# Two blocks in one kernel: layer-norm sums on ScalarE, lower parts and routing in another order, four experts combined on the chip

## The chip, the cores and the metric

The kernel runs on one core of a Trainium2 chip, in one launch. The metric is device microseconds of one execution; shown is the median of three runs. The engines are TensorE (PE in the rows, its weight loads PEld), VectorE (DVE), ScalarE (ACT), GpSimd (POOL) and SyncE (SP, which issues most of the DMAs). Arrays are 128 partitions by columns.

## The reference

512 tokens of 1024 numbers pass through two transformer blocks. Block 1 ends with two layer norms and a mixture of 16 experts between them; block 2 is an attention block with RMS norms and ends with 32 experts.

```python
# block 1, from its attention on
x = layer_norm(ALPHA * x + mixed, ln1_g[l], ln1_b[l])
ffn = hier_moe(x, ...)                       # 16 experts, 2 for a token
x = layer_norm(ALPHA * x + ffn, ln2_g[l], ln2_b[l])

def layer_norm(x, g, b):
    mu = jnp.mean(xf, -1, keepdims=True)
    var = jnp.mean(jnp.square(xf - mu), -1, keepdims=True)
    return ((xf - mu) * lax.rsqrt(var + LN_EPS)) * g + b

# block 2, its experts, on hf = rms_norm(x)
    e_p, e_i = lax.top_k(softmax(el_sel), 2)         # within the best group
    combine = jnp.sum(one_hot(expert_idx, 32) * weights[..., None], axis=1)
    for e in range(32):
        he = jax.nn.silu(hf @ w_gate[e]) * (hf @ w_up[e])
        y = y + combine[:, e:e + 1] * (he @ w_down[e])
```

## The kernel before

The tokens stand in four tiles of 128 (t = 0 to 3). Dense products at full precision split both operands into a high part (`whi`, `xh`, made by ScalarE) and a lower part (`wlo`, `xl`: the number less its high part, made by VectorE or GpSimd), and sum three products. A scheduler that models times sets the order of each engine's instructions when the kernel is built; the code sets what depends on what, and `issue_after` ties one piece of code behind another.

*Block 1's head of the experts.* `block1_out` gives the four tiles of the first norm's input; `done(t)` in `run` calls `layernorm` on each (two statistics of 512 columns and an aggregate on VectorE, L750 and L752; the root on GpSimd; shift, gain and bias on VectorE, L756 and L759) and then `moe_tile`, which transposes the tile, computes the routing logits and chooses experts (`choose`, L876 to L893) and ranks tokens in each expert (`slot`).

*Entering block 2.* `enter2` takes each tile's sum of expert results out of PSUM (`combined`, L1271), calls `layernorm` on it (the second norm), then makes the RMS-normed row (`hrow`: sum of squares on ScalarE L1780, scaling on VectorE L1782), transposes it and splits it into `hhi` and `hlo`, the operand of block 2's first products.

*Block 2's head of the experts.* For each tile, `rows(t)` makes the normed row (`frow`, L1915), its high part `xh` (L1916) and its lower part `xl` (L1918, GpSimd), and `choose` takes the logits (`lg`), masks (`og`, `ml`), the two best experts (`top`, `m`, `rm`, `Mb`) and, with a product on TensorE, the token's place in its expert (`slot`, L914). `moe_experts_rows` then makes, for four experts at a time, selection masks from `slot` (`select`, L1150), gathers those tokens by matmuls with the masks (`gather`, L1164), and calls `moe_route`, which turns the choices into weights and lists (`gd`, `gp`, `Aw`, `e`, `w`, `mxa`, `wts`, `ra`).

*Block 2's experts.* Each expert has four gate-up quarters and two down halves of 512 KB, loaded by SyncE in the order of use (`more`, L823). A load goes into a buffer that an earlier one has freed, and waits until at most four are under way (`FLIGHT`). `gu(e)` multiplies the gathered tokens by the quarters (L1179) and makes `gul`; `htr` transposes two experts' `gul` at a time into `hT`; `down(e)` multiplies by the halves (L1208). The result `yy` (three buffers, scaled by ScalarE L1218 or VectorE L1220) is added to the token rows in DRAM, `xa`, by an indirect DMA of GpSimd (L1221), one after another, since each adds to the same array.

*The last two experts* (`LAST` = 2) are not scattered. Their results stay on the chip as high and lower halves (`spare`, L1213 and L1214), and matmuls with selection masks made by `tokens` bring them to their rows (`combined`, L1271). Once the last scatter, expert 29's, has landed, SyncE loads the four tiles of `xa` (L1227, `self.base`); VectorE adds the matmuls' sums (L1253), and the rows are written out. Buffers for all this (`spare`) are weight buffers that `more` holds back near the end (`self.free`).

Of the kernel before, what the change touches and what calls it, by code (L numbers as in the profile page):

```python
# [11 lines left out]
F32 = mybir.dt.float32  # L12
F32R = mybir.dt.float32r
BF = mybir.dt.bfloat16
I32 = mybir.dt.int32
AF = mybir.ActivationFunctionType
OP = mybir.AluOpType
# [3 lines left out]
P = 128  # L21
S = 512
D = 1024
NT = S // P
# [30 lines left out]
class Kern:  # L55
# [686 lines left out]
                   (self.topk(), 48, 5, 24), (self.dsa(), 36, 11, 39), (self.ssd(), 14, 23, 37), (self.residual(), 1, 30, 31))  # L742
        self.flush()

    def layernorm(self, xt, out, pool, gb, step=D):

        nc = self.nc
        st = pool.tile([P, 2, 6], F32, tag="bn", name="bn", bufs=2)
        for i in range(2):
            nc.vector.bn_stats(st[:, i, :], xt[i])  # L750
        mv = pool.tile([P, 4], F32, tag="mv", name="mv", bufs=2)
        nc.vector.bn_aggr(mv[:, 0:2], st)  # L752
        r = self.rsqrt(mv[:, 3:4], mv[:, 1:2], 1.0, 1e-5, 1)
        for i in range(2):
            s = slice(i * 512, (i + 1) * 512)
            nc.vector.scalar_tensor_tensor(out[:, s], xt[i], mv[:, 0:1], gb[0][:, s], op0=OP.subtract, op1=OP.mult)  # L756
        for c in range(0, D, step):
            s = slice(c, c + step)
            nc.vector.scalar_tensor_tensor(out[:, s], out[:, s], mv[:, 3:4], gb[1][:, s], op0=OP.mult, op1=OP.add)  # L759
        return r  # L760
# [40 lines left out]
    def more(self):  # L801


        n = len(self.places)
        while len(self.place) < len(self.seq):
            i = len(self.place)
            if i < n:
                pool, tag = self.places[i]
            else:
                while self.rows is None and self.place[self.prev][0] is None:  # L810
                    self.prev += 1
                if self.used <= self.prev:
                    return
                pool, tag = self.place[self.prev]
                self.prev += 1
                if pool is self.mw and len(self.free) < self.LAST and len(self.seq) - i <= 14:
                    self.free.append((pool, tag))
                    continue
            self.place.append((pool, tag))
            e, c = self.seq[i]  # L820
            raw = tag if pool is None else pool.tile([P, 1024], F32, tag=tag, name="raw", bufs=1)
            self.raws[e, c] = raw
            ld = self.nc.sync.dma_start(raw, self.wd[e, c - 4] if c > 3 else self.wgu[e, c])  # L823
            self.loads.append(ld.ins)
            under = self.FLIGHT if i >= n else self.FIRST
            if i >= under:
                self.tc.add_manual_dep(ld.ins, self.loads[i - under].name,
                                       mybir.DependencyInfo(mybir.DependencyClass.Sync, mybir.DependencyReason.DATA), reason="few under way")
# [298 lines left out]
    def moe_experts_rows(self, me):  # L1127


        nc, E, T, V, rows, bank = self.nc, self.E, self.T_, self.nc.vector, self.rows, self.bank  # L1130
        sels, xes, sgs, hTs = {}, {}, {}, {}
# [2 lines left out]

        def tokens():

            st = [self.spare(F32R)[:, :S] for _ in range(LAST)]
            sh = me.tile([2 * T, LAST, NT], F32, name="sh")
            for t in range(NT):
                V.tensor_scalar(sh[:, :, t], self.sl[:, 0, E - LAST:], -128.0 * t, None, op0=OP.add)  # L1140
            for e in range(LAST):
                for t in range(NT):
                    V.tensor_scalar(st[e][:, t * P:(t + 1) * P], self.c("iota"), sh[:, e, t:t + 1], None, op0=OP.is_equal)
            return st

        def select(e):

            if e < E:
                sels[e] = me.tile([P, NT, 4, T], F32R, tag="sel", name="sel", bufs=2)
                V.tensor_tensor(sels[e], self.c("iota")[:, None, None, :T].to_broadcast([P, NT, 4, T]),  # L1150
                                self.slot[:, :, e:e + 4, None].to_broadcast([P, NT, 4, T]), op=OP.is_equal)
                xes[e] = me.tile([P, KT, 4, T], F32, tag="xe", name="xe", bufs=2)

        def gather(e, q):


            if e >= E:
                return
            pg = bank("pv")
            m = [(t, part) for t in range(NT) for part in rows]  # L1160
            for j in range(2):
                c = slice((2 * q + j) * P, (2 * q + j + 1) * P)
                for i, (t, part) in enumerate(m):
                    nc.tensor.matmul(pg[:, j * 256:(j + 1) * 256], part[t][:, c], sels[e][:, t].rearrange("p e s -> p (e s)"),  # L1164
                                     start=(i == 0), stop=(i == len(m) - 1))
            o = xes[e][:, 2 * q:2 * q + 2].rearrange("p k e s -> p (k e s)")
            if q % 2:
                nc.scalar.activation(o, pg, AF.Copy)
            else:
                V.tensor_copy(o, pg)  # L1170
# [27 lines left out]
        def down(e):  # L1198
# [24 lines left out]
            if e == E - LAST - 1:  # L1223
                self.base = []
                for t in range(NT):
                    self.base.append(self.spare())
                    self.order = [nc.sync.dma_start(self.base[t], self.xa[t * P:(t + 1) * P, :])]  # L1227

        select(0)
        for q in range(4):  # L1230
            gather(0, q)
        self.moe_route(me)
        for p in range(E // 2 + 1):
            e = 2 * p
            if e == E - 4:
                st = tokens()
            if e % 4 == 0:
                select(e + 4)
            for i in range(2):
                if e < E:  # L1240
                    gu(e + i)
                down(e + i - 2)
            if e < E:
                for q in range(2):
                    gather(e - e % 4 + 4, e % 4 + q)
                htr(p)
        for t in range(NT):
            x = self.base[t]
# [545 lines left out]
    def enter2(self, hp, hT, gains):  # L1794

        nc = self.nc
        gb2, gb = gains[0:2], gains[2]
        for t in range(NT):
            xs = self.accs[t] if t < 2 else self.first_part(t)
            for n in range(2):  # L1800
                self.combined(xs[n], t, n, slice(-1, None), False)
            x = hp.tile([P, D], F32, tag="x", name="x", bufs=3)
            self.layernorm(xs, x, hp, gb2, 512)
            nc.gpsimd.dma_start(self.xr[t * P:(t + 1) * P, :], x)
            row = self.rms_row(x, hp, gb, "hrow")
            for h in range(2):
                tp = self.bank("tp")
                for k in range(4):
                    self.transpose(tp[:, k * P:(k + 1) * P], row[:, (4 * h + k) * P:(4 * h + k + 1) * P])
                sl = (slice(None), slice(4 * h, 4 * h + 4), slice(t * P, (t + 1) * P))  # L1810
                self.hilo(hT[0][sl], hT[1][sl], tp.rearrange("p (k c) -> p k c", k=4))

    def run(self, stage=99):
        tc, nc, A = self.tc, self.nc, self.A
# [23 lines left out]
        rt = mws.enter_context(right("rt1"))  # L1838
# [6 lines left out]
        gb = self.pp.tile([P, 2, D], F32, name="gb")  # L1845
        bcast(gb, "ln1", 2 * D)

        def done(t):
            x = self.xr_[t]
            self.order = [self.layernorm([x[:, 0:512], x[:, 512:]], x, rt, (gb[:, 0], gb[:, 1]), 512 if t == NT - 1 else D)]  # L1850
            self.later(lambda: self.moe_tile(t, x), 2)
        for _ in self.block1_out(1, done):
            self.more()
# [19 lines left out]
            return  # L1873
        self.NG, self.NNAT, self.NPR, self.NATW = 6, 4, 7, 512
        nmw, nme = 19, 1
        self.LAST = 2
        self.NX, self.NY, self.FLIGHT = 0, 3, 4
        self.FIRST = 3
        xs, xl, short = [], [], ExitStack()
# [17 lines left out]
        rt, xh = self.rt, self.rows[0]  # L1897
# [9 lines left out]
        def rows(t):  # L1907

            x, s_ = xs[t], ss[:, t]
            nc.vector.tensor_scalar(s_[:, 2:3], s_[:, 0:1], s_[:, 1:2], 1.0 / D, op0=OP.add, op1=OP.mult)  # L1910
            nc.vector.tensor_scalar(s_[:, 2:3], s_[:, 2:3], 1e-6, None, op0=OP.add)
            nc.gpsimd.tensor_tensor(s_[:, 3:4], s_[:, 2:3], self.mh[:, 0:1], op=OP.pow)
            nc.gpsimd.dma_start(self.xa[t * P:(t + 1) * P, :], x)
            row = xp.tile([P, D], F32, tag="frow", name="frow", bufs=1)
            nc.vector.scalar_tensor_tensor(row, x, s_[:, 3:4], gf, op0=OP.mult, op1=OP.mult)  # L1915
            a = nc.scalar.activation(xh[t], row, AF.Copy)  # L1916
            xl.append(rt.tile([P, D], F32R, tag=f"xo{t}", name="xl"))
            b = nc.gpsimd.tensor_tensor(xl[t], row, xh[t].bitcast(F32), op=OP.subtract)  # L1918
            self.order = [a, b]

        def ev(t, p, u):
# [187 lines left out]
```

## Time and profile before

| | us |
|---|---|
| median of three runs | 1411.08 (1409.53 to 1414.77) |
| profiled execution | 1408.74 |
| its span in the profile | 1407.0 |
| TensorE busy | 1303.7 (93%) |
| VectorE busy | 774.0 (55%) |
| ScalarE busy | 591.6 (42%) |
| GpSimd busy | 452.1 (32%) |

The span is the time from the first to the last instruction that the profile shows; 1.74 us of the execution lie around it. The stretches spoken of below are, in us from the span's start: block 1's head of the experts (228 to 297), entering block 2 (464 to 500), block 2's head of the experts (1080 to 1125), its experts while TensorE is never idle (1125 to 1330) and the end (1330 to 1407). A busy share over the whole span says little on a change that touches these stretches; what each engine does and waits for within one is read from its timeline.

### The profile page before, as it was taken

To read this page: it belongs to the slowest core of one execution; us is meant where nothing else is said; L and a number is where in the kernel's file an instruction comes from. 1 tells how busy PE (TensorE), PEld (TensorE's weight loads), DVE (VectorE), ACT (ScalarE), POOL (GpSimd) and SP (SyncE) were. 2 spreads that over 40 slices of the span, in tenths; PEclk is the share of its full clock that TensorE was granted. 3 is DMA by queue.
4 is the path that set the end of the run, shared out by engine and by line. 5 is a ranking of instruction groups with operands and counts; after the bars stand their busy time and mean duration, and the time that the engine had idled before them with its cause. 6 is when DMAs were issued, how large, how long until landed. Compare 5 with 4: busy or idle time off the path is not lost.

```text
span 1407.0 us, 21509 instructions
## 1 busy us (share of the span) xinstructions
PE 1303.7 (93%) x8172; PEld 998.5 (71%) x8188; DVE 774.0 (55%) x1659; ACT 591.6 (42%) x1235; POOL 452.1 (32%) x368
## 2 busy tenths in 40 slices
PE   8898999869999798999999999999999799999983
PEld 8876777746665597987899999887789644545421
DVE  6899964858785856665455354224553723322222
ACT  5466442336664346654654354444223212221110
POOL 3354642422220336531143243123632302111211
PEclk9999999879999999999999999999999899999987
DMA  6122114889997211201121222226328589999994
GB/s 238 60 76 75 46 39 170 304 295 305 313 302 283 98 46 63 109 34 61 50 79 69 76 70 75 100 76 230 114 96 326 184 299 381 356 366 363 377 373 154
DMA packets 69124, 250.77 MB, mean 178 GB/s; under 512 B 12370, under 2 KB 12626, under 8 KB 62864
## 3 DMA queue, kind: packets, MB, share of 16 engines
q1 hardware_dynamic: 56304, 220.64, 43.2%
q0 software_dynamic: 11408, 25.24, 6.6%
q10 hardware_dynamic: 1296, 3.38, 0.6%
q8 instruction: 68, 1.11, 0.3%
q14 instruction: 48, 0.39, 0.1%
HBM read 230.29 MB, written 26.71 MB: 183 GB/s over the span
## 4 chain that ended last, share of the span: by engine, by line
PE 76%; DVE 13%; DMA 5%; ACT 2%; issue 2%; POOL 1%; SPq 0%; DVEq 0%; ACTq 0%; POOLq 0%
PE mm L181 13%; PE mm L183 13%; PE mm L182 13%; PE mm L1179 8%; PE tp L266 5%; PE pv L1164 5%; PE sc L1208 3%; DMA xa<-yy,idx 2%; PE pv L1759 2%; PE mm L1051 2%; DVE work L409 1%; DVE m L408 1%; PE sc L1733 1%; PE sc L1489 1%; DVE pr L707 1%
## 5 line engine op out<-in xcount | busy, mean ns | idle before, releaser
L154 POOL TENSOR_TENSOR wlo<-raw,whi 128x1024 fp32r<-128x1024 f32 (+4 forms) x62 | 149.6, 2416 | 252.5 <-ACT whi L153 231.9
L153 ACT ACTIVATE whi<-raw 128x1024 fp32r<-128x1024 f32 (+4 forms) x172 | 178.3, 1039 | 99.3 <-PE mm L183 42.4
L154 DVE TENSOR_TENSOR wlo<-raw,whi 128x1024 fp32r<-128x1024 f32 (+3 forms) x110 | 142.6, 1297 | 103.8 <-ACT whi L153 103.3
L1221 POOL DMA_INDIRECT xa<-yy,idx x30 | 46.4, 1548 | 220.3 <-DMA xa<-yy,idx 136.5
L183 PE MATMUL mm<-whi,hRl 128*128 128x256 f32 x384 | 108.8, 284 | 0.0
L181 PE MATMUL mm<-whi,hhi 128*128 128x256 f32 (+2 forms) x352 | 102.8, 292 | 4.8 <-ACT qraw L1428 1.8
L181 PE MATMUL mm<-whi,hRh 128*128 128x256 f32 x352 | 102.6, 292 | 0.0
L183 PE MATMUL mm<-whi,hlo 128*128 128x256 f32 (+2 forms) x352 | 101.5, 288 | 0.0
L182 PE MATMUL mm<-wlo,hhi 128*128 128x256 f32 (+2 forms) x352 | 101.0, 287 | 0.0
L1179 PE MATMUL mm<-raw,xe 128*64 128x512 f32 x396 | 100.6, 610 | 0.0
L182 PE MATMUL mm<-wlo,hRh 128*128 128x256 f32 x352 | 99.8, 283 | 0.0
L271 POOL TENSOR_TENSOR hss<-hss,mh 128x4 f32<-128x4 f32 (+1 forms) x64 | 60.1, 940 | 100.2 <-DVE hss L270 89.8
L181 PEld LDWEIGHTS mm<-whi,hhi 128*128 128x128 f32 x352 | 68.5, 195 | 10.5 <-issue 3.8
L183 PEld LDWEIGHTS mm<-whi,hRl 128*128 128x128 f32 x384 | 73.2, 191 | 0.0
L1186 DVE TENSOR_TENSOR gul<-gul,mm 64x512 f32<-64x512 f32 x32 | 21.9, 686 | 92.4 <-ACT gul L1185 92.4
L182 PEld LDWEIGHTS mm<-wlo,hhi 128*128 128x128 f32 x352 | 68.6, 195 | 1.6 <-issue 1.4
L183 PEld LDWEIGHTS mm<-whi,hlo 128*128 128x128 f32 x352 | 68.3, 194 | 1.4 <-issue 1.1
L1164 PEld LDWEIGHTS pv<-sel,xh 128*128 128x128 f32 x256 | 49.8, 194 | 27.2 <-issue 20.6
L1164 PE MATMUL pv<-sel,xh 128*128 128x256 f32 x256 | 67.1, 297 | 1.8 <-issue 1.8
L181 PEld LDWEIGHTS mm<-whi,hRh 128*128 128x128 f32 x352 | 67.2, 191 | 0.2
L182 PEld LDWEIGHTS mm<-wlo,hRh 128*128 128x128 f32 x352 | 67.2, 191 | 0.0
L1164 PE MATMUL pv<-sel,xl 128*128 128x256 f32 x256 | 65.6, 292 | 0.0
(537 smaller groups left out, 3634.4 us busy)
## 6 DMA issues: line engine op xcount, KB each, us to landing
raw<-in_wgu SPq DMA_DIRECT2D x163, 512.0 KB
raw<-in_wd SPq DMA_DIRECT2D x77, 512.0 KB
raw<-in_w2b SPq DMA_DIRECT2D x26, 1024.0 KB
rawp<-in_wgu SPq DMA_DIRECT2D x29, 512.0 KB
raw<-in_wo SPq DMA_DIRECT2D x12, 1024.0 KB
rawp<-in_wd SPq DMA_DIRECT2D x19, 512.0 KB
raw<-in_w1b SPq DMA_DIRECT2D x8, 1024.0 KB
spare<-xa SPq DMA_DIRECT2D x8, 512.0 KB
```

What stands on the lines that cost most here:

```text
L153: self.nc.scalar.activation(hi[:, :n], src, AF.Copy)
L154: eng.tensor_tensor(lo[:, :n], src, hi[:, :n].bitcast(F32), op=OP.subtract)
L181: nc.tensor.matmul(ps, lh, rh, start=start and i == 0, stop=False)
L182: nc.tensor.matmul(ps, lh, rl, start=False, stop=False)
L183: nc.tensor.matmul(ps, ll, rh, start=False, stop=stop and i == n - 1)
L266: self.nc.tensor.transpose(out, in_, self.c("ident")[:n, :n])
L271: return self.nc.gpsimd.tensor_tensor(out, out, self.mh[:, :n], op=OP.pow)
L1051: nc.tensor.matmul(pg[:T, :], x[2][:, j, :], wf[:, j * 512:(j + 1) * 512], start=False, stop=(j == 1))
L1164: nc.tensor.matmul(pg[:, j * 256:(j + 1) * 256], part[t][:, c], sels[e][:, t].rearrange("p e s -> p (e s)"), start=(i == 0), stop=(i == le ...
L1179: nc.tensor.matmul(pg[j * T:(j + 1) * T], x[:, 2 * c + j, e % 4], w[:, j * 512:(j + 1) * 512], start=(c == 0), stop=(c == 3))
L1208: nc.tensor.matmul(py[n * T:(n + 1) * T], hT[:, k, :], w[:, n * 512:(n + 1) * 512], start=(k == 0), stop=(k == 1))
L1221: nc.gpsimd.indirect_dma_start(out=xa2, out_offset=bass.IndirectOffsetOnAxis(ap=self.idx[:, 0, e:e + 1], axis=0), in_=y, in_offset=None, b ...
```

## The change

There are four edits.

1. `layernorm` gets a second form, used for tiles 0 to 2 of the first norm and tiles 1 to 3 of the second: ScalarE sums the two half rows (a copy with accumulator each), VectorE makes the negative mean of them, ScalarE sums the squares of the shifted half rows, VectorE makes the variance.
2. `LAST` becomes 4 in block 2: experts 28 to 31 stay on the chip and are combined by matmuls, 64 instead of 32, and 28 instead of 30 experts are scattered. As many weight buffers as before are held back (`LAST // 2`), and `tokens` packs two masks into a buffer.
3. `moe_route` is issued after the first selection masks.
4. The lower part `xl` in block 2's head is made by VectorE.

The loads of `xa` follow expert 27's scatter, since with edit 2 that is the last one.

```diff
@@ layernorm
-    def layernorm(self, xt, out, pool, gb, step=D):
+    def layernorm(self, xt, out, pool, gb, step=D, sums=None):
...
+            for i in range(2):
+                nc.scalar.activation(sums, xt[i], AF.Copy, accum_out=st[:, i, 0:1])
+            nc.vector.tensor_scalar(mv[:, 0:1], st[:, 0, 0:1], st[:, 1, 0:1], -1.0 / D, op0=OP.add, op1=OP.mult)
+            for i in range(2):
+                nc.scalar.activation(sums, xt[i], AF.Square, bias=mv[:, 0:1], accum_out=st[:, i, 1:2])
+            nc.vector.tensor_scalar(mv[:, 1:2], st[:, 0, 1:2], st[:, 1, 1:2], 1.0 / D, op0=OP.add, op1=OP.mult)
+            r = self.rsqrt(mv[:, 3:4], mv[:, 1:2], 1.0, 1e-5, 1)
+            shift = OP.add
...
@@ more
-                if pool is self.mw and len(self.free) < self.LAST and len(self.seq) - i <= 14:
+                if pool is self.mw and len(self.free) < (self.LAST if self.rows is None else self.LAST // 2) and len(self.seq) - i <= 14:
@@ moe_experts_rows
-            st = [self.spare(F32R)[:, :S] for _ in range(LAST)]
+            st = [self.spare(F32R) for _ in range(LAST // 2)]
+            st = [st[i // 2][:, i % 2 * S:(i % 2 + 1) * S] for i in range(LAST)]
...
-        select(0)
+        chosen = select(0)
         for q in range(4):
             gather(0, q)
-        self.moe_route(me)
+        with self.tc.issue_after(chosen.ins):
+            self.moe_route(me)
@@ enter2
-            self.layernorm(xs, x, hp, gb2, 512)
+            self.layernorm(xs, x, hp, gb2, 512, hp.tile([P, 512], BF, tag="sums", name="sums", bufs=1) if t else None)
@@ run
-            self.order = [self.layernorm([x[:, 0:512], x[:, 512:]], x, rt, (gb[:, 0], gb[:, 1]), 512 if t == NT - 1 else D)]
+            last = t == NT - 1
+            sums = None if last else self.pp.tile([P, 512], BF, tag="sums", name="sums", bufs=1)
+            self.order = [self.layernorm([x[:, 0:512], x[:, 512:]], x, rt, (gb[:, 0], gb[:, 1]), 512 if last else D, sums)]
...
-        self.LAST = 2
+        self.LAST = 4
...
-            b = nc.gpsimd.tensor_tensor(xl[t], row, xh[t].bitcast(F32), op=OP.subtract)
+            b = nc.vector.tensor_tensor(xl[t], row, xh[t].bitcast(F32), op=OP.subtract)
```

The scheduler moves more than these lines. Three places follow, the order before and then the new one.

SyncE at the end: the last weight loads (gate-up quarters `in_wgu`, down halves `in_wd`) and the loads of the sums (`spare<-xa`), before:

```order
L823 DMA raw<-in_wd 128x1024
L823 DMA rawp<-in_wd 128x1024
L823 DMA rawp<-in_wgu 128x1024
L823 DMA rawp<-in_wd 128x1024
L823 DMA rawp<-in_wgu 128x1024
L823 DMA rawp<-in_wd 128x1024 x2
L823 DMA raw<-in_wd 128x1024
L823 DMA rawp<-in_wd 128x1024
L1227 DMA spare<-xa 128x1024 x4
L1261 DMA out_dram<-spare 128x1024
```

and after:

```order
L834 DMA raw<-in_wd 128x1024
L834 DMA rawp<-in_wd 128x1024
L834 DMA rawp<-in_wgu 128x1024
L1240 DMA spare<-xa 128x1024 x3
L834 DMA rawp<-in_wd 128x1024
L1240 DMA spare<-xa 128x1024
L834 DMA rawp<-in_wgu 128x1024
L834 DMA rawp<-in_wd 128x1024 x2
L834 DMA raw<-in_wd 128x1024
L834 DMA rawp<-in_wd 128x1024
L1275 DMA out_dram<-spare 128x1024
```

The loads of the sums, which stood behind the last weight load, now stand ahead of six of them, three of the four together ahead of the first.

VectorE in block 2's head, from the last tile's choice to the first selection masks (`sel`), before:

```order
L889 MAX top<-ml 128x8
L890 COPY m_10984<-top 128x2
L892 MATCH_REPLACE rm<-m_10984,ml 128x40
L924 TENSOR_TENSOR Aw<-ml,m_10984 128x128
L977 TENSOR_TENSOR e_12118<-m_10984 128x4
L893 TENSOR_SCALAR Mb<-rm 128x32
L925 TENSOR_TENSOR Aw<-Aw,cf 128x128
L979 TENSOR_SCALAR w_12119<-e_12118 128x4
L914 SCALAR_TENSOR_TENSOR slot<-mm,Mb 128x128
L926 TENSOR_REDUCE mxa<-Aw 128x4
L980 RECIPROCAL w_12119<-w_12119 128x4
L1150 TENSOR_TENSOR sel<-cf,slot 128x1024
```

and after:

```order
L896 TENSOR_SCALAR og<-og,mx 128x4
L1934 TENSOR_TENSOR xl<-frow,xh 128x1024
L904 TENSOR_SCALAR Mb<-rm 128x32
L897 TENSOR_TENSOR ml<-lg,og 128x32
L900 MAX top<-ml 128x8
L901 COPY m_11008<-top 128x2
L903 MATCH_REPLACE rm<-m_11008,ml 128x40
L904 TENSOR_SCALAR Mb<-rm 128x32
L925 SCALAR_TENSOR_TENSOR slot<-mm,Mb 128x128
L1162 TENSOR_TENSOR sel<-cf,slot 128x1024
```

The routing rows (`Aw`, `e`, `w`, `mxa`) are gone from between the choice and `sel`, and the last tile's lower part `xl` stands ahead of its mask `ml`.

TensorE at the end: the down products (L1208, then L1221), gate-up products (L1179, then L1192) of the last experts, the transposes of `gul` and the first combining matmuls (`spare`), before:

```order
L1179 MATMUL mm<-rawp,xe 64x512 x2
L1208 MATMUL sc<-rawp,hT 64x512 x2
L1179 MATMUL mm<-rawp,xe 64x512 x2
L266 MATMUL tp<-cf,gul 128x128 x2
L1208 MATMUL sc<-rawp,hT 64x512 x4
L1208 MATMUL sc<-raw,hT 64x512 x2
L1208 MATMUL sc<-rawp,hT 64x512 x2
L1271 MATMUL sc<-spare 128x512
```

and after:

```order
L1192 MATMUL mm<-rawp,xe 64x512 x2
L1285 MATMUL pv<-spare 128x512
L1285 MATMUL mm<-spare 128x512
L1285 MATMUL pv<-spare 128x512
L1285 MATMUL mm<-spare 128x512 x4
L266 MATMUL tp<-cf,gul 128x128 x2
L1285 MATMUL tp<-spare 128x512 x4
L1221 MATMUL sc<-rawp,hT 64x512 x6
```

Combining matmuls for experts 28 and 29 now stand between the last gate-up and down products; the down products of experts 30 and 31 still come behind the transposes of `gul`.

## Rows read from the trace of the kernel before

**Rows 1.** The page's part 4: the chain that ended last, its shares by engine.
```profile
PE 76%; DVE 13%; DMA 5%; ACT 2%; issue 2%; POOL 1%; SPq 0%; DVEq 0%; ACTq 0%; POOLq 0%
```

**Rows 2.** Stretches: PE, PEld, DVE, ACT, POOL busy us, PEclk, DMA share, GB/s.
```profile
464.00:500.00 36.00, 27.15 (x137) 21.47 (x137) 29.90 (x61) 11.25 (x23) 11.06 (x15) 0.87 0.22 83
1080.00:1125.00 45.00, 34.71 (x288) 33.66 (x287) 31.40 (x89) 11.58 (x21) 15.22 (x13) 0.85 0.57 201
1125.00:1330.00 205.00, 205.00 (x1116) 101.45 (x1115) 59.55 (x108) 42.36 (x78) 34.08 (x22) 1.00 0.99 357
1330.00:1390.00 60.00, 46.49 (x202) 16.66 (x200) 14.09 (x27) 10.62 (x20) 12.36 (x8) 0.89 0.81 280
```

**Rows 3.** VectorE's timeline in block 1's head: start us, us, line, operation.
```profile
267.81 0.41 DVE L716 SCALAR_TENSOR_TENSOR xr<-xr,mm 128x256 f32<-128x256 f32 x1
...
268.25 0.69 DVE L750 BATCH_NORM_STATS2 bn<-xr 128x6 f32<-128x512 f32 x1
268.98 0.21 DVE L752 BATCH_NORM_AGGREGATE mv<-bn 128x2 f32<-128x12 f32 x1
269.22 0.15 DVE L270 TENSOR_SCALAR mv<-mv 128x1 f32<-128x1 f32 x1
```

**Rows 4.** TensorE's timeline there.
```profile
264.45 0.29 PE L183 MATMUL mm<-whi,clo 128*128 128x256 f32 x1
```

**Rows 5.** ScalarE's timeline where block 2 is entered.
```profile
475.53 1.06 ACT L1780 ACTIVATE hrow<-x 128x1024 f32<-128x1024 f32 x1 [10.54 <-DVE x L759]
```

**Rows 6.** ScalarE's timeline in block 2's head.
```profile
1087.39 0.63 ACT L1927 ACTIVATE fsq<-xo 128x512 bf16<-128x512 f32 x1 [2.36 <-DVE xo L1923]
1087.93 0.19 ACT L1927 ACTIVATION_READ_ACCUMULATOR fsq<-xo 128x1 f32 x1
```

**Rows 7.** GpSimd's timeline in block 2's head.
```profile
1108.70 2.34 POOL L1918 TENSOR_TENSOR xl<-frow,xh 128x1024 fp32r<-128x1024 f32 x1 [2.89 <-ACT xh L1916]
```

**Rows 8.** VectorE's timeline in block 2's head.
```profile
1105.19 0.19 DVE L886 TENSOR_TENSOR ml<-lg,og 128x32 f32<-128x32 f32 x1
...
1108.85 2.23 DVE L886 TENSOR_TENSOR ml<-lg,og 128x32 f32<-128x32 f32 x1
...
1112.46 0.29 DVE L914 SCALAR_TENSOR_TENSOR slot<-mm,Mb 128x128 f32<-128x128 f32 x1
```

**Rows 9.** The page's part 5: VectorE's 1024-column subtractions.
```profile
L154 DVE TENSOR_TENSOR wlo<-raw,whi 128x1024 fp32r<-128x1024 f32 (+3 forms) x110 | 142.6, 1297 | 103.8 <-ACT whi L153 103.3
```

**Rows 10.** The chain that ended last, in order of time: start, us, what.
```profile
1360.91 7.49 DMA xa<-yy,idx
...
1375.73 3.69 DMA xa<-yy,idx
...
1384.90 3.75 DMA xa<-yy,idx
...
1390.34 7.94 DMA spare<-xa
```

**Rows 11.** SyncE's timeline at the end.
```profile
1360.77 0.33 SPq L823 DMA_DIRECT2D rawp<-in_wgu  x1
...
1369.57 0.33 SPq L823 DMA_DIRECT2D rawp<-in_wd  x1
1388.71 2.01 SPq L1227 DMA_DIRECT2D spare<-xa  x4
```

**Rows 12.** TensorE's timeline at the end.
```profile
1374.65 1.02 PE L1179 MATMUL mm<-rawp,xe 128*64 128x512 f32 x4
...
1379.03 3.31 PE L1208 MATMUL sc<-rawp,hT 128*64 128x512 f32 x8 [0.52 <-DVE hT L1196]
...
1388.50 0.39 PE L1271 MATMUL mm<-spare 64*128 64x512 f32 x1
```

**Rows 13.** VectorE's timeline at the end.
```profile
1383.98 1.61 DVE L1214 SCALAR_TENSOR_TENSOR spare<-sc,gs,spare 128x512 fp32r<-128x512 f32 x2 [5.00 <-ACT spare L1213]
1392.05 0.69 DVE L1253 TENSOR_TENSOR spare<-spare,sc 128x512 f32<-128x512 f32 x1 [6.46 <-DMA spare<-xa]
```

More of the change, by code (lines that the diff above doesn't have):

```diff
@@ L743, in block1 @@
         self.flush()
-    def layernorm(self, xt, out, pool, gb, step=D):
+    def layernorm(self, xt, out, pool, gb, step=D, sums=None):
         nc = self.nc
         st = pool.tile([P, 2, 6], F32, tag="bn", name="bn", bufs=2)
-        for i in range(2):
-            nc.vector.bn_stats(st[:, i, :], xt[i])
         mv = pool.tile([P, 4], F32, tag="mv", name="mv", bufs=2)
-        nc.vector.bn_aggr(mv[:, 0:2], st)
-        r = self.rsqrt(mv[:, 3:4], mv[:, 1:2], 1.0, 1e-5, 1)
+        if sums is None:
+            for i in range(2):
+                nc.vector.bn_stats(st[:, i, :], xt[i])
+            nc.vector.bn_aggr(mv[:, 0:2], st)
+            r = self.rsqrt(mv[:, 3:4], mv[:, 1:2], 1.0, 1e-5, 1)
+            shift = OP.subtract
+        else:
+            for i in range(2):
+                nc.scalar.activation(sums, xt[i], AF.Copy, accum_out=st[:, i, 0:1])
+            nc.vector.tensor_scalar(mv[:, 0:1], st[:, 0, 0:1], st[:, 1, 0:1], -1.0 / D, op0=OP.add, op1=OP.mult)
+            for i in range(2):
+                nc.scalar.activation(sums, xt[i], AF.Square, bias=mv[:, 0:1], accum_out=st[:, i, 1:2])
+            nc.vector.tensor_scalar(mv[:, 1:2], st[:, 0, 1:2], st[:, 1, 1:2], 1.0 / D, op0=OP.add, op1=OP.mult)
+            r = self.rsqrt(mv[:, 3:4], mv[:, 1:2], 1.0, 1e-5, 1)
+            shift = OP.add
         for i in range(2):
             s = slice(i * 512, (i + 1) * 512)
-            nc.vector.scalar_tensor_tensor(out[:, s], xt[i], mv[:, 0:1], gb[0][:, s], op0=OP.subtract, op1=OP.mult)
+            nc.vector.scalar_tensor_tensor(out[:, s], xt[i], mv[:, 0:1], gb[0][:, s], op0=shift, op1=OP.mult)
         for c in range(0, D, step):
@@ L1149, in select @@
                 sels[e] = me.tile([P, NT, 4, T], F32R, tag="sel", name="sel", bufs=2)
-                V.tensor_tensor(sels[e], self.c("iota")[:, None, None, :T].to_broadcast([P, NT, 4, T]),
-                                self.slot[:, :, e:e + 4, None].to_broadcast([P, NT, 4, T]), op=OP.is_equal)
+                chosen = V.tensor_tensor(sels[e], self.c("iota")[:, None, None, :T].to_broadcast([P, NT, 4, T]),
+                                         self.slot[:, :, e:e + 4, None].to_broadcast([P, NT, 4, T]), op=OP.is_equal)
                 xes[e] = me.tile([P, KT, 4, T], F32, tag="xe", name="xe", bufs=2)
+                return chosen
         def gather(e, q):
```

## The prediction

> **What bounds the kernel now.** I read the chain's shares first: TensorE carries 76% of it, VectorE 13%, DMA 5% [rows 1]. So a microsecond taken from another engine counts only in a stretch where TensorE stands still. The table by stretch says where that is [rows 2]. Where block 2 is entered TensorE is busy 27.15 of 36 us while VectorE is busy 29.90: VectorE sets the pace. In block 2's head it is 34.71 of 45, at a granted clock of 0.85, with VectorE at 31.40. From 1125 to 1330 TensorE is busy for all of its 205 us, and the DMA share is 0.99: whatever is won ahead of that is handed on unchanged, and nothing done within it shows. After 1330 TensorE is busy 46.49 of 60. There the chain is the serial scatter of the expert results into DRAM [rows 10], and behind it SyncE's four loads of the sums, issued at 1388.71 [rows 11]. The reader should take two things from this: edits 1, 3 and 4 act in three heads where VectorE is late; edit 2 acts on a tail made of scatter, load, add, write.
>
> **Layer norms in block 1's head.** For three tiles VectorE loses two statistics of 0.69 and an aggregate of 0.21, and gains two column operations of 0.15 [rows 3]: 1.59 − 0.30 = 1.29 us a tile, 3.9 in all. ScalarE gains four half-row passes; the nearest row is the square with accumulator, 0.63 + 0.19 [rows 6], so 3.28 a tile. Of the tile's own chain this makes 3.6 where 1.6 stood, 2.0 more. What can be won is seen on the last tile, which keeps the old form: its matmuls end at 264.45 + 0.29 = 264.74 [rows 4], VectorE takes them up at 267.81 [rows 3], 3.07 late. All of it is the best end; 2.0 lost, if the longer chain is the one waited for, the worst. VectorE's queue ahead of that row also holds work that stays, so I take half: **−1.5 us**.
>
> **Layer norms where block 2 is entered.** The same for three tiles: 3.9 us off a VectorE that is nearly always busy there, onto a ScalarE that just before sat idle for 10.54 us [rows 2, 5]. ScalarE's twelve passes at 0.82 are 9.8 us, which fit in that hole only in part, since the sums of the later tiles come when it also makes the rows and their high parts; the longer chain is again 2.0. Bounds −3.9 and +2.0. Half of the best end, as TensorE waits for the first rows and these get only part of it: **−2.0 us**.
>
> **Block 2's head.** The lower part moves from GpSimd, 2.34 us [rows 7], to VectorE, where the like subtraction takes 1.30 [rows 9]. While GpSimd's ran, VectorE's small operation `ml` took 2.23 instead of the 0.19 of another tile [rows 8]: the two engines hold each other up, so 2.04 comes back and 1.30 is paid, 0.74 on the last tile's path. For the two tiles before it I count half, 0.74 together. The routing rows leave the way of `slot` and the first selection (nine small rows, six of them in the order shown above, by some 0.17 each near the column operation's 0.15 [rows 3]; half of them filled a wait): 0.75. Sum **−2.2 us**, bounds −4 (all three holds on the path, and the power that was queued behind them) and +1 (VectorE now does 4 × 1.30 = 5.2 more in a stretch where it is the late engine). `slot` starts at 1112.46 [rows 8], and should start about 2 us earlier against the head's begin.
>
> GpSimd's shared port is a rule of the Trainium skill too, and it names what the change newly puts on VectorE: GPSIMD Engine Reference, Specifications, has contention with VectorE instructions "in a 2-port perf mode or with two SBUF inputs". By it the moved subtraction, with two such inputs, could be held as `ml` was, which would lose the 0.74; but the only long GpSimd operation in that head is the one that goes, so the sum stays.
>
> **The tail.** Two effects. First, experts 28 to 31 instead of 30 and 31 are combined by TensorE: 32 more matmuls at about 0.13 us (32 took from 1384.9 to 1388.9 [rows 12]), 4 us, most of it while TensorE waits. Two scatters go, and they went last: the chain ends with expert 27's, 9.2 us sooner on unchanged spacing (1384.90 − 1375.73 [rows 10]). Second, the price: in the order of SyncE the loads of the sums no longer stand behind the last weight load but ahead of six of them (one down half of expert 29, the last gate-up quarter of 31, the four downs of 30 and 31). The sums wait for expert 27's scatter. SyncE therefore stops there, with these six queued behind. The wait itself was harmless before, with nothing but the sums behind it: SyncE stood from 1369.9 to 1388.71 [rows 11].
>
> That a waiting DMA holds its queue follows from DMA: Bandwidth & Descriptors, Anatomy of one DMA: any semaphore wait "happens on the issuing sequencer before dispatch". The idle SyncE in the rows agrees, but no row has transfers queued behind; without the rule the tail would be rival A's, −8.0.
>
> I count this in the times of before; the earlier gains come off afterwards. SyncE's last load ahead of the wait goes out at 1360.77 [rows 11]. At 357 GB/s a load of 512 KB takes 1.47 us [rows 2], four in flight 5.9: the stream is dry at about 1366.7. Scatters then run at the unloaded spacing of 4.6 instead of 8.2 (1360.91 + 7.49 against 3.69 and 3.75 [rows 10]). Expert 25's lands at 1366.7, so 26's starts at 1367.6, 27's at 1372.2 and lands 3.75 later: T0 = 1375.9 (1373.8 if 25 also runs free; 1379.42 as it was, 1375.73 + 3.69). From there: the first load lands 3.34 after its issue (1392.05 − 1388.71 [rows 11, 13]); the needed gate-up quarter is the sixth issued, 5 × 1.47 later; its matmuls take 1.02, the way to the first down matmul 3.36 (1375.67 to 1379.03), down to the end of the lower half 6.56 (to 1383.98 + 1.61), the combining matmuls left 3.3 (to 1388.89), four adds of 0.69 behind them, and the write 7.34 (the last sum lands at 1390.34 + 7.94 = 1398.28, two adds, span end 1407.0) [rows 10, 12, 13]. That is T0 + 35.0 = 1410.9 where it was 1407.0: **+3.9 us**. Ends: 1373.8 gives +1.8; 1379.42 with loads at the sums' own spacing of 2.08 (1392.05 to 1398.28 in three) gives +10.5.
>
> The selection masks (eight more column operations) and the evacuations of two more results lie beside a VectorE busy 59.55 of 205 us [rows 2]: nothing; without that cover, about 2 us.
>
> **Sum.** −1.5 − 2.0 − 2.2 + 3.9 = −1.8 us on the profiled execution of 1408.74, so 1406.9. It is 2.3 below the median of the runs, 1411.08; against that the forecast is **1409 us**.
>
> **The rivals.**
> A, *the two scatters are simply saved.* If the scatters keep up with the experts, SyncE finds expert 27 landed when it arrives and nothing is blocked. TensorE's end then decides: lower half at 1385.59, + 3.3 + 2.76 + 7.34 = 1399.0, −8.0, with the heads −13.7: 1397. For it: two of the last links go. Against it: expert 25's scatter was only starting at 1360.91, when SyncE arrives [rows 10, 11]. The Trainium skill speaks for it: DMA: Bandwidth & Descriptors, Anatomy of one DMA, fits 2.0 us plus bytes over 436 GB/s, 2.6 for 256 KB, at which the chain would never lag; the rows show 3.69 alone and 7.49 beside the stream.
>
> B, *slower: the block at its full price.* The wait for expert 27 stays at 1379.42 and the six loads share the DMA engines with the four sums at 2.08 each: +10.5 − 5.7 = +4.8, 1416. It ends on the slow side once the gate-up quarter lands later than 1388.4 in before's times (1407.0 + 5.7 − 24.3); I have 1386.6. TensorE's idle of over 10 us and a low clock behind it, as in the head (0.85), push that way.
>
> C, *the longer norm chains are what is waited for.* Then both norm terms turn to +2.0, the heads together to +1.8, and with the tail +5.7: 1417. For it: on ScalarE the sums stand ahead of rows and high parts that TensorE waits for. Against: its idle 10.54 [rows 5].
>
> **How the numbers follow.** Forecast 0.50, A 0.20, B 0.18, C 0.12. Measurement can tell about 0.5%, 7 us. Faster: A, and 0.08 of the forecast where the heads give their best ends (−11 + 1.8): 0.28. Slower: 0.07 of B (heads under half of what I count), 0.05 of C, 0.02 of the forecast: 0.14. The rest, 0.58, is no change. Range: from 1398, which leaves out about half of A, to 1419, which leaves out the upper parts of B and C; 0.2 lie outside.
>
> **What would show it.** Right, if in the new profile SyncE waits 10 us or more at the loads of the sums with weight loads after it, DMA runs dry before that, and TensorE stands still ahead of expert 31's last gate-up quarter; if VectorE's operations in block 2's head have no 2 us holds and `slot` comes about 2 us sooner; and if the last expert's scatter and the first experts start some 6 us earlier. Wrong, if SyncE's wait is short (A), if the quarter lands over 13 us after the scatter (B), or if TensorE waits for `hhi` behind ScalarE's sums where block 2 is entered (C).

## The result

The changed kernel takes 1421.15 us (median of 17 runs, 1415.21 to 1427.47) against 1408.32 us before (17 runs, 1405.06 to 1414.77): a ratio of 1.0085, 95% interval 1.0069 to 1.0100. It is 12.8 us slower by the medians, 12.0 by the ratio, where 1409 us was forecast, no change, in a range that ended at 1419. Single executions of either kernel spread over some 10 us, and the profiled one of the new kernel is its slowest, 1427.47 us with a span of 1425.7; so stretches are compared below, not whole spans. Line numbers are those of each kernel, which an edit shifts.

The profile after, the page's parts 1 and 4 (busy us; the chain's shares):

```profile
PE 1321.7 (93%) x8220; PEld 1010.5 (71%) x8220; DVE 764.6 (54%) x1666; ACT 608.6 (43%) x1284; POOL 435.1 (31%) x362
...
PE 66%; DMA 15%; DVE 13%; issue 3%; ACT 2%; POOL 1%; SPq 0%; POOLq 0%; DVEq 0%; ACTq 0%
```

DMA's share of the chain has gone from 5% [rows 1] to 15%, TensorE's from 76% to 66%. The chain now leads through the scatters, a weight load and the combining matmuls. SyncE's timeline at the end (start us, us, line, operation), the answer to [rows 11]:

```profile
1369.67 0.33 SPq L834 DMA_DIRECT2D rawp<-in_wgu  x1
1383.50 1.28 SPq L1240 DMA_DIRECT2D spare<-xa  x3
1384.83 0.42 SPq L834 DMA_DIRECT2D rawp<-in_wd  x1
1385.34 0.50 SPq L1240 DMA_DIRECT2D spare<-xa  x1
1385.89 0.45 SPq L834 DMA_DIRECT2D rawp<-in_wgu  x1
1386.39 1.72 SPq L834 DMA_DIRECT2D rawp<-in_wd  x2
1392.74 0.33 SPq L834 DMA_DIRECT2D raw<-in_wd  x1
1395.29 0.33 SPq L834 DMA_DIRECT2D rawp<-in_wd  x1
```

and SyncE's waits from 1330 on (us in total, times, longest):

```profile
SPq L1240 <- DMA xa<-yy,idx: 13.4, 1, 13.4
```

From 1370 to 1383.50 SyncE issues nothing; it waits for expert 27's scatter with six weight loads behind it. TensorE's timeline there, for [rows 12]:

```profile
1382.42 0.39 PE L1285 MATMUL pv<-spare 64*128 64x512 f32 x1
1392.72 1.98 PE L1221 MATMUL sc<-rawp,hT 128*64 128x512 f32 x4 [9.91 <-DMA rawp<-in_wd]
...
1396.63 1.97 PE L1192 MATMUL mm<-rawp,xe 128*64 128x512 f32 x4
...
1400.02 2.07 PE L1285 MATMUL mm<-spare 64*128 64x512 f32 x4 [0.27 <-DVE gul L1199]
1402.03 0.69 PE L266 MATMUL tp<-cf,gul 128*128 128x128 f32 x2
1402.64 2.07 PE L1285 MATMUL tp<-spare 64*128 64x512 f32 x4
1404.65 3.92 PE L1221 MATMUL sc<-rawp,hT 128*64 128x512 f32 x12
```

and the stretches around it, with the columns of [rows 2]:

```profile
1330.00:1370.00 40.00, 30.50 (x142) 9.83 (x138) 13.08 (x33) 8.10 (x15) 7.74 (x5) 0.99 1.01 366
1370.00:1384.00 14.00, 12.80 (x44) 3.92 (x44) 2.27 (x4) 1.70 (x3) 3.11 (x2) 0.78 0.43 117
1384.00:1404.00 20.00, 10.22 (x23) 4.19 (x24) 2.29 (x4) 1.69 (x3) 0.00 (x0) 0.56 0.68 262
1404.00:1426.00 22.00, 11.65 (x62) 6.67 (x60) 6.37 (x10) 1.38 (x2) 0.00 (x0) 0.73 0.26 99
```

The weight stream, at 366 GB/s until 1370, falls to 117. TensorE waits 9.91 us for the down half of expert 29. From 1384 to 1404 the granted clock is 0.56, close to the lower of its two levels (0.50, which is 1.2 GHz): four gate-up matmuls take 1.97 us instead of 1.02 [rows 12].

Ahead of the tail three more stretches changed. Since start and clock vary from run to run, the table gives stretches between fixed events, in us from the traces of all kernels, one profiled execution each: a is from the first expert matmul of block 1 to the first scaled `cn` of block 2 (a tile of its attention; a holds the second norm), b from there to the first `xo` taken out of PSUM (block 2's attention, which no edit touches), c from there to the first selection mask (the head).

| kernel | a | b | c |
|---|---|---|---|
| before | 201.3 | 551.9 | 61.9 |
| after | 200.0 | 557.3 | 59.9 |
| after, loads of the sums last (`e1_loads_last`) | 200.3 | 557.4 | 60.0 |
| after, two experts combined (`e2_last2`) | 199.7 | 557.2 | 59.9 |
| after, loads of the sums on GpSimd (`e4_loads_pool`) | 200.0 | 557.5 | 59.4 |
| before, edit 2 (`e3_only4`) | 201.3 | 551.6 | 61.9 |
| before, sums in block 1's norm (`n1_ln1`) | 203.6 | 553.6 | 62.1 |
| before, sums in the second norm (`n2_ln2`) | 198.7 | 551.8 | 62.1 |
| before, sums in both (`n12_both`) | 200.3 | 557.3 | 61.8 |
| before, edits 3 and 4 (`h_head`) | 202.5 | 551.8 | 59.7 |
| before, edit 2, loads last (`e5_only4_last`) | 202.0 | 551.9 | 63.9 |
| second norm, edits 2 to 4, loads last (`b2_best`) | 200.1 | 551.7 | 59.9 |

By this table the second norm and the head win what they were meant to win, about 2 us each. Block 2's attention loses 5.5 wherever both norms are changed.

Two finer cuts change how a and b read: the first `kn` that GpSimd makes, some 35 us into b, and the end of a wait of TensorE for `dv`, a tile of ScalarE, near 694 (both are tiles of the attention).

| kernels | first expert matmul to `kn` | `kn` to `dv` | `dv` to first `xo` |
|---|---|---|---|
| before | 237.0 | 159.6 | 356.6 |
| `n2_ln2` | 234.4 | 159.6 | 356.5 |
| `e3_only4`, `h_head`, `e5_only4_last` | 235.4 to 236.4 | 159.6 | 357.9 to 358.2 |
| `b2_best` | 234.2 | 159.6 | 358.0 |
| `n1_ln1` | 237.0 | 162.3 | 357.9 |
| after, `e1_loads_last`, `e2_last2`, `e4_loads_pool`, `n12_both` | 235.3 to 235.9 | 163.6 to 163.7 | 357.9 to 358.2 |

So 4.1 of the 5.5 us go with both norms changed, and 1.4 also go in kernels whose norms are before's. `e3_only4`, `h_head`, `e5_only4_last` and `b2_best` lose these 1.4 too; their b is before's only because 1.5 to 1.7 us come off between `cn` and `kn`. Measured to `kn`, the second norm wins 1.2 us (236.4 the mean of five kernels with its old form, 235.3 of seven with the new); by stretch a it is 2.3.

### The profile page after: what moved, and what is told of

The parts are those of the page before. It is cut to its first block, busy times and chain, and to the rows that moved or that the text cites. A ratio compares the mean times of both kernels' runs of the same rounds, so it can differ in the third digit from the quotient of the medians.

```text
span 1425.7 us, 21637 instructions
## 1 busy us (share of the span) xinstructions
PE 1321.7 (93%) x8220; PEld 1010.5 (71%) x8220; DVE 764.6 (54%) x1666; ACT 608.6 (43%) x1284; POOL 435.1 (31%) x362
## 4 chain that ended last, share of the span: by engine, by line
PE 66%; DMA 15%; DVE 13%; issue 3%; ACT 2%; POOL 1%; SPq 0%; POOLq 0%; DVEq 0%; ACTq 0%
PE mm L181 13%; PE mm L183 13%; PE mm L182 13%; DMA xa<-yy,idx 11%; PE tp L266 5%; PE mm L1192 3%; PE pv L1177 2%; PE pv L1773 2%; PE mm L1062 2%; DVE work L409 2%; PE sc L1221 1%; DVE m L408 1%; PE sc L1503 1%; PE sc L1747 1%; DVE pr L707 1%
## 5 line engine op out<-in xcount | busy, mean ns | idle before, releaser
L1234 POOL DMA_INDIRECT xa<-yy,idx x28 | 43.5, 1554 | 211.7 <-DMA xa<-yy,idx 119.9
L1192 PE MATMUL mm<-raw,xe 128*64 128x512 f32 x396 | 101.6, 622 | 3.5 <-DVE xe L1183 3.5
```

The costliest lines, as they stand in the source:

```text
L1192: nc.tensor.matmul(pg[j * T:(j + 1) * T], x[:, 2 * c + j, e % 4], w[:, j * 512:(j + 1) * 512], start=(c == 0), stop=(c == 3))
L1234: nc.gpsimd.indirect_dma_start(out=xa2, out_offset=bass.IndirectOffsetOnAxis(ap=self.idx[:, 0, e:e + 1], axis=0), in_=y, in_offset=None, b ...
```

## The experiments

Theory 1 held that SyncE's order makes the loss; theory 2 that the heads and norms make it, since in the profile SyncE's last load ahead of the wait went out 8.9 us later than before. Ratios are to the kernel before on the same chips; the changed kernel's 1421.15 comes from another set of runs, and the kernel before has medians of 1408.1 to 1409.8 over the sets.

**The loads of the sums behind the last weight load.**

```diff
+            if e == E - 1:
+                self.base = []
...
+                with ExitStack() as behind:
+                    for ld in self.loads[-8:]:
+                        behind.enter_context(self.tc.issue_after(ld))
+                    for t in range(NT):
+                        self.base.append(self.spare())
...
-            if e == E - LAST - 1:
-                self.base = []
...
```

> The changed kernel with the four loads of the sums issued behind the last weight load on SyncE; nothing else differs. Theory 1 (SyncE's order makes the loss: the six weight loads behind a wait): expert 27's scatter lands about where it did before (1379.4), TensorE ends as before (1389), and the tail is 8 us shorter than before's: about 1398 us, 10 us under before and 23 under the changed kernel. Theory 2 (the heads and norms make the loss; SyncE's last load ahead of the wait went out 8.9 us later than before): only the tail's part comes back, about 1408 us, the same as before.

Measured 1403.51 us, ratio 0.9958 (0.9936 to 0.9980): 17.6 under the changed kernel, 4.6 under before. The order alone is worth more than the whole loss. Theory 1 was 5 us too hopeful. It took the heads' gain for granted, and stretch b is 557.4 here too; and the sums go out at 1387.41 in the profile, 1.3 us sooner than before [rows 11], not at 1379.4, as the scatters run beside the stream to its end.

**Two experts combined, the rest as changed.**

```diff
-        self.LAST = 4
+        self.LAST = 2
```

> The changed kernel with two experts combined on the chip instead of four (edit 2 undone; norms, lower parts and routing as changed). Theory 1: the heads keep their small gain, before minus 2 to 5 us, about 1404. Theory 2: before plus 5 to 9 us, 1413 to 1417.

Measured 1411.66 us, ratio 1.0023 (1.0001 to 1.0045). Neither: edits 1, 3 and 4 together lose 3.6 us by the medians (0.1 to 6.3 by the interval), where 5.7 were to be won. So a second cause remains, small beside the tail's.

**Edit 2 alone** (against the kernel before, with the masks packed and the buffers held as in the change).

```diff
...
-        self.LAST = 2
+        self.LAST = 4
```

> The kernel before with edit 2 alone: four experts combined on the chip, the loads of the sums where the scheduler puts them, ahead of six weight loads. Theory 1: all of the loss and the heads' gain not there to offset it, before plus 14 to 17 us, about 1424. Theory 2: a small part of the loss, before plus 3 to 5 us, about 1412.

Measured 1421.45 us (four runs), ratio 1.0085 (1.0051 to 1.0118): 13.3 us by the medians, 12.0 by the ratio, the whole loss from edit 2 by itself. With the heads of before, GpSimd's timeline shows the last two scatters, and SyncE's timeline the stop:

```profile
1371.23 1.56 POOL L1222 DMA_INDIRECT xa<-yy,idx  x1 [7.10 <-DVE gul L1187]
1375.68 1.55 POOL L1222 DMA_INDIRECT xa<-yy,idx  x1 [2.89 <-DMA xa<-yy,idx]
```

```profile
1366.33 0.33 SPq L823 DMA_DIRECT2D rawp<-in_wgu  x1
1379.36 1.28 SPq L1228 DMA_DIRECT2D spare<-xa  x3
```

Expert 27's scatter starts at 1375.68, where it did before [rows 10], and SyncE stands 12.7 us. From SyncE's release to the end of the span 42.4 us pass (1379.36 to 1421.8), in the changed kernel 42.2 (1383.50 to 1425.7).

**The loads of the sums on GpSimd.**

```diff
-                    self.order = [nc.sync.dma_start(self.base[t], self.xa[t * P:(t + 1) * P, :])]
+                    self.order = [nc.gpsimd.dma_start(self.base[t], self.xa[t * P:(t + 1) * P, :])]
```

> The changed kernel with the loads of the sums issued by GpSimd behind its last scatter, so that SyncE's weight loads wait for nothing. Theory 1: as with the loads behind the last weight load, about 1398 us, or 1 us less. Theory 2: about 1408 us.

Measured 1406.15 us, ratio 0.9981 (0.9963 to 1.0000): 15 under the changed kernel. Theory 1's 1398 was missed by 8, 5.5 of them the attention's. What matters is that nothing stands behind the waiting load, not which queue it is on.

That left the 5.5 us in the attention. Four profiles with both norms changed have them, two without do not, and no edit touches that code. Theory 3: the scheduler, which orders by modelled times, puts the attention in another order once the norms' times have moved. Theory 4: the sums themselves, by when work arrives.

**Sums in block 1's norm alone.**

```diff
-            self.layernorm(xs, x, hp, gb2, 512, hp.tile([P, 512], BF, tag="sums", name="sums", bufs=1) if t else None)
+            self.layernorm(xs, x, hp, gb2, 512)
```

(against the changed kernel, with edits 2 to 4 undone.)

> The kernel before with ScalarE's sums in block 1's norm alone. So far: in the four profiles with both norms changed, block 2's attention (from the first scaled `cn`, 499, to the first `xo` taken out of PSUM, 1051) takes 557.4 us instead of 551.8, and TensorE's granted clock falls to 0.58 to 0.84 at 540 to 550. Theory 3 (the scheduler, whose modelled times the norms moved, orders the attention otherwise; this loses 5.6): the attention's order is another one here too, so that stretch takes 3 to 6 us more, and the whole is before plus 2 to 5. Theory 4 (the sums themselves, by the time at which work arrives, whatever the order): the same, with half the loss for half the sums.

Measured 1413.45 us, ratio 1.0026 (1.0009 to 1.0044). The attention's order is a third one; it takes 1.7 us more, and stretch a 2.3 more. By the finer cuts nothing is lost up to `kn` (237.0 us, as before), 2.7 from there to `dv` and 1.3 behind it. This alone fits both theories.

**Sums in the second norm alone.**

```diff
-            last = t == NT - 1
-            sums = None if last else self.pp.tile([P, 512], BF, tag="sums", name="sums", bufs=1)
-            self.order = [self.layernorm([x[:, 0:512], x[:, 512:]], x, rt, (gb[:, 0], gb[:, 1]), 512 if last else D, sums)]
+            self.order = [self.layernorm([x[:, 0:512], x[:, 512:]], x, rt, (gb[:, 0], gb[:, 1]), 512 if t == NT - 1 else D)]
```

(against the changed kernel, with edits 2 to 4 undone.)

> The kernel before with ScalarE's sums in the second norm alone. Here the scheduler leaves the attention in before's order. Theory 3: that stretch takes before's 551.8 us, the stretch ahead of it (first expert of block 1 to `cn`) 1.3 us less, the whole is before minus 1 to 2 us. Theory 4: the attention takes 3 to 6 us more, the whole is before plus 2 to 4.

Measured 1406.38 us, ratio 0.9978 (0.9957 to 0.9998). The order is before's, b is 551.8, and a is 2.6 less. Theory 4 falls for the second norm. For block 1's, sums and order changed together in every kernel.

**The head's two edits alone** (against the kernel before).

```diff
-            b = nc.gpsimd.tensor_tensor(xl[t], row, xh[t].bitcast(F32), op=OP.subtract)
+            b = nc.vector.tensor_tensor(xl[t], row, xh[t].bitcast(F32), op=OP.subtract)
...
-        select(0)
+        chosen = select(0)
...
-        self.moe_route(me)
+        with self.tc.issue_after(chosen.ins):
+            self.moe_route(me)
```

> The kernel before with edits 3 and 4 alone (routing behind the selection masks, lower parts on VectorE). Both theories: the stretch from the first `xo` to the first selection mask takes 59.8 us instead of 61.9, the whole is before minus 2 us. If the whole is the same within 0.5 us, the gain is lost again in the experts, which are then bound by their weight loads and not by their start.

Measured 1407.98 us, ratio 0.9993 (0.9977 to 1.0009). The stretch is as expected, 59.7; for the whole the interval takes in both a gain of 2 and none, so whether it reaches the end by itself stays open.

**Both norms alone.**

```diff
-    def layernorm(self, xt, out, pool, gb, step=D):
+    def layernorm(self, xt, out, pool, gb, step=D, sums=None):
...
```

(against the kernel before, with the second form and its callers; no other edit.)

> The kernel before with edit 1 alone, ScalarE's sums in both norms; the scheduler gives the attention the changed kernel's order. Theory 3: the attention's stretch takes 557.4 us instead of 551.8, with TensorE's granted clock down near 540 to 550, the norms' own stretches win 1 to 2, the whole is before plus 3 to 5 us (1412 to 1413). If the attention's loss belongs to edits 2 to 4, the whole is before minus 1 to 3.

Measured 1411.20 us, ratio 1.0006 (0.9986 to 1.0026). The attention takes 557.3 with the clock down, as theory 3 says, so the loss belongs to edit 1 (4.1 us of it by the finer cuts); the whole is only 1.4 us slower than before, under the 3 to 5 expected, though the interval reaches 3.7.

**Edit 2 with the loads last** (against the kernel before).

```diff
...
-        self.LAST = 2
+        self.LAST = 4
...
+                with ExitStack() as behind:
+                    for ld in self.loads[-8:]:
+                        behind.enter_context(self.tc.issue_after(ld))
...
```

> The kernel before with edit 2 alone and the loads of the sums behind the last weight load. If the tail's gain is 8 us as reckoned in rival A and adds to the norm's and head's 3.4 in the best kernel (1396.4), this one is at 1400 us, 8 under before. If the two lean on each other (an earlier start only helps with a shorter tail), it is at 1402 to 1404.

Measured 1401.68 us, ratio 0.9957 (0.9934 to 0.9979): 8.1 us by the medians, 6.1 by the ratio (3.0 to 9.3). The tail's gain is close to rival A's and is there without the heads.

**The best of it: second norm, edits 2 to 4, loads last** (against the changed kernel).

```diff
-            last = t == NT - 1
-            sums = None if last else self.pp.tile([P, 512], BF, tag="sums", name="sums", bufs=1)
-            self.order = [self.layernorm([x[:, 0:512], x[:, 512:]], x, rt, (gb[:, 0], gb[:, 1]), 512 if last else D, sums)]
+            self.order = [self.layernorm([x[:, 0:512], x[:, 512:]], x, rt, (gb[:, 0], gb[:, 1]), 512 if t == NT - 1 else D)]
...
+                with ExitStack() as behind:
+                    for ld in self.loads[-8:]:
+                        behind.enter_context(self.tc.issue_after(ld))
...
```

> The kernel before with ScalarE's sums in the second norm, edits 2, 3 and 4, and the loads of the sums behind the last weight load; block 1's norm as before, so that the attention keeps before's order. Theory 3: minus 8 (tail), 1.3 (norm) and 2 (head): about 1397 us, 6 under the changed kernel with the loads behind the weights. Theory 4: no better than that one, 1403.

Measured 1396.42 us, ratio 0.9908 (0.9885 to 0.9931): 12.6 us under before and 24.7 under the changed kernel, as the sum of the parts said. SyncE's and TensorE's end in it:

```profile
1362.18 4.81 SPq L834 DMA_DIRECT2D rawp<-in_wd  x4
1367.99 0.33 SPq L834 DMA_DIRECT2D raw<-in_wd  x1
1377.23 1.76 SPq L1226 DMA_DIRECT2D spare<-xa  x4
```

```profile
1361.00:1377.00 16.00, 14.57 (x66) 5.26 (x62) 2.95 (x5) 2.77 (x5) 3.11 (x2) 1.00 0.79 278
```

All weight loads are out at 1368.3, SyncE waits 8.9 us with nothing behind it, and TensorE works at full clock to the last expert.

## Why the prediction was wrong

**The tail: right mechanism, wrong size.** What was forecast is in the profile: SyncE stops, DMA runs dry, TensorE stands ahead of the blocked loads. The term was +3.9 us and measures +13.3 (`e3_only4`; 12.0 by the ratio). Two steps of it failed, the second by more.

- *T0.* I let SyncE reach the wait at 1361 and the scatters run free from 1366.7, so that expert 27's would land at 1375.9. In `e3_only4` SyncE stopped only at 1366.7, expert 25's scatter ran beside the stream (1362.59 to 1370.50), and expert 27's landed at 1379.4: my worst end, 1379.42. Part of this is that one execution. Its weight loads are 0.4 us behind those of before at 1111 and 5.6 behind at SyncE's stop, and in `h_head`, without edit 2, they fall back by 3.9 on the same way; from the stop to T0 it is 12.7 us, less than my 14.8. By the medians T0 has some 2 us of the miss (13.3 − 3.9 − 7.4).
- *T0 + 35.0.* It is 42.2. In the changed kernel the gate-up quarter lands at T0 + 11.7 (1395.23), and its matmuls begin at T0 + 13.1 (1396.63) instead of 10.7: in TensorE's order the down half of expert 29 and combining matmuls stand ahead of them. The quarter's matmuls take 1.97 instead of 1.02, and the way to the next down matmul 6.05 (1398.60 to 1404.65) instead of 3.36, because two rows of four combining matmuls at the lower clock, 2.07 us each, stand around the transposes. The last part, lower half to last add, took 7.1 instead of 6.1. I had taken all of these from rows in which TensorE had just worked, and here they stand behind ten idle microseconds. The new order was in front of me, with these matmuls between.

Rival B was this mechanism, at +10.5, and named the clock as the push; I gave it 0.18. Of its loads at 2.08 us each: the fourth one issued landed at T0 + 9.2 (1392.72), near B's 9.6 and over my 7.8, so the pace was nearer to B's; the rest is TensorE's order and clock. Of my signs, SyncE's wait, the dry stream and TensorE's standstill came true, though TensorE stood ahead of expert 29's down half and not yet of the quarter. The last scatter was to start some 6 us earlier; it starts at 1379.70, where expert 27's started at 1375.73 [rows 10].

**The heads.** Block 2's head: −2.2 forecast, −2.1 measured (61.9 to 59.8, leaving out `e5_only4_last` with the old head at 63.9). VectorE's timeline there, for [rows 8]:

```profile
1114.83 1.22 DVE L1934 TENSOR_TENSOR xl<-frow,xh 128x1024 fp32r<-128x1024 f32 x1
...
1116.05 0.18 DVE L897 TENSOR_TENSOR ml<-lg,og 128x32 f32<-128x32 f32 x1
...
1117.47 0.29 DVE L925 SCALAR_TENSOR_TENSOR slot<-mm,Mb 128x128 f32<-128x128 f32 x1 [0.28 <-PE mm L923]
```

`ml` is back at 0.18 us and the moved subtraction takes 1.22, not held by anything. Whether GpSimd's shared port (the Trainium skill, GPSIMD Engine Reference, Specifications) could hold it, as weighed ahead, this head cannot show: GpSimd has nothing over 0.6 us beside it. That this gain reaches the end is not shown either (`h_head`).

The second norm: −2.0 forecast, −2.3 measured by stretch a (202.1 the mean of five kernels with the old form, 199.9 of seven with the new), −1.2 by the cut at `kn`. Six of ScalarE's twelve passes lie in the hole of [rows 5]; its timeline behind that shows others, and the wait for `hhi`'s input:

```profile
478.09 0.67 ACT L761 ACTIVATE sums<-sc,mv 128x512 bf16<-128x512 f32 x1
478.66 0.19 ACT L761 ACTIVATION_READ_ACCUMULATOR sums<-sc,mv 128x1 f32 x1
...
482.69 0.60 ACT L173 ACTIVATE hhi<-tp 128x512 fp32r<-128x512 f32 x1 [0.69 <-PE tp L266]
```

A shifted square costs 0.67 + 0.19, close to the 0.82 that I took. Rival C's wait for `hhi` did not become the bound: from 464 to 500 TensorE waits for `hrow`, `hlo`, `cn` and `x`, but not for `hhi`.

Block 1's norm: −1.5 forecast, no gain seen. The first expert matmul comes at 298.5 on the mean of six kernels with the old form (297.3 to 300.6) and at 298.9 with the new (296.9 to 300.7).

**What had no term at all: the attention, +5.5.** I compared the orders at the places of the edits and not between them. The times that the norms take in the scheduler's model moved, and 40 to 80 us later it ordered the attention otherwise. TensorE's timeline at the third group of transposes of `kn`, before:

```profile
540.54 0.27 PE L181 MATMUL mm<-whi,hhi 128*128 128x192 f32 x1
542.12 0.64 PE L266 MATMUL tp<-cf,kn 128*96 128x128 f32 x4 [1.30 <-POOL kn L1457]
542.51 0.34 PE L182 MATMUL mm<-wlo,hhi 128*128 128x192 f32 x1
```

and after:

```profile
541.00 0.27 PE L181 MATMUL mm<-whi,hhi 128*128 128x192 f32 x1
543.57 1.09 PE L266 MATMUL tp<-cf,kn 128*96 128x128 f32 x4 [2.30 <-POOL kn L1471]
```

Before, TensorE fills the wait for GpSimd's `kn` with products of the next weights until 540.81 and stands 1.30 us. After, it has fewer of them ahead of the transposes and stands 2.30 us; from there the granted clock falls. From 540 to 545, with the columns of [rows 2], in the kernels before, after, `n12_both` and `n2_ln2`:

```profile
540.00:545.00 5.00, 3.70 (x31) 3.40 (x30) 2.96 (x12) 2.93 (x7) 3.81 (x5) 1.00 0.00 0
```

```profile
540.00:545.00 5.00, 2.70 (x18) 2.44 (x17) 2.50 (x8) 2.37 (x5) 3.67 (x4) 0.84 0.00 0
```

```profile
540.00:545.00 5.00, 4.98 (x24) 4.93 (x25) 2.74 (x13) 2.10 (x6) 2.65 (x4) 0.50 0.00 0
```

```profile
540.00:545.00 5.00, 4.39 (x30) 3.71 (x30) 4.19 (x15) 4.00 (x9) 2.65 (x5) 1.00 0.00 2
```

The clock is 1.00 in the six kernels with before's order there, and 0.50 to 0.84 in the five with the new one; the wait is 1.30 us in the six and 2.30 in the five. In `e1_loads_last` it is 0.58 from 540 to 545, 0.73 to 550 and 1.00 to 560, so (0.42 + 0.27) × 5 = 3.4 us of full clock are missing, an estimate of the most that the clock can have of the 4.1 us lost by 579. How much the order would cost at full clock was not tried.

The last 1.4 us are the clock's without a new order. At the wait for `dv` the order of TensorE's instructions is the same in all twelve kernels for the 20 us on either side, and so is the wait, 1.44 to 1.46 us. Behind it the clock stays at 1.00 in the kernel before and in `n2_ln2`, and falls in the other ten. TensorE's timeline and the 5 us behind it (columns of [rows 2]), before:

```profile
694.44 0.39 PE L181 MATMUL mm<-whi,hRmk 128*128 128x256 f32 x1 [1.46 <-ACT dv L1698]
```

```profile
694.40:699.40 5.00, 4.96 (x41) 4.96 (x42) 3.15 (x8) 5.00 (x8) 1.89 (x1) 1.00 0.02 3
```

and in `e3_only4`, whose norms are before's:

```profile
693.47 0.39 PE L181 MATMUL mm<-whi,hRmk 128*128 128x256 f32 x1 [1.45 <-ACT dv L1699]
```

```profile
693.40:698.40 5.00, 4.93 (x28) 4.93 (x29) 3.21 (x9) 5.00 (x8) 1.86 (x1) 0.66 0.01 3
```

Why the clock falls in the one and not in the other is open.

**The sum.** Block 1's norm 0, the second −2.3, the attention +5.5, the head −2.1, the tail +13.3 make +14.4; measured +12.8. Forecast were −1.5, −2.0, 0, −2.2 and +3.9. The tail's size alone would have turned the sign, and so would the attention.

## What to carry to other kernels

Before a load that waits goes into a queue, list what stands behind it and who needs that; then price the stall at the clock that the waiting engine will have after it, with its queue as it now stands, not with durations from before. Where a scheduler sets the order by modelled times, compare the orders over the whole program: an edit can cost more in code that it doesn't touch than it wins in its own. And a part that wins by itself may belong in the kernel though the whole change loses: the parts sorted out here make 1396 us of 1421.

## What the runs showed of the hardware

A scatter of 128 × 512 sums lands 3.7 to 3.9 us after its start when the weight stream rests and 5.9 to 9.2 beside it, in the kernels before and after; that is what ties the tail to the stream. The Trainium skill's fit for such a queue (DMA: Bandwidth & Descriptors, Anatomy of one DMA), 2.6 us for that size, is under both; here the measurement decides.

One microsecond more of standing still, 2.30 instead of 1.30 between busy stretches, went with a fall of TensorE's granted clock from 1.00 to between 0.50 and 0.84 over the next 5 us, in five kernels out of five; I had counted a wait of that size as its length only. The length alone does not decide: behind the same wait of 1.45 us in the same order the clock fell in ten kernels of twelve, and from there to the first `xo` these ten took 1.3 to 1.7 us longer.
